# Two-layer diffusion backbone: the softmax scale moves, sign included, into the query copies; the second layer's gate products move to other steps

## The chip, the cores and the metric

One core of a Trainium2 chip runs the whole program. The time is device microseconds of one execution, as the median of several. The engines are TensorE (PE in the profile; its weight loads are PEld), VectorE (DVE), ScalarE (ACT), GpSimd (POOL) and SyncE (SP, which issues most of the transfers).

## What is computed

Two trunk layers over 512 latent and 128 context tokens, model width 1024, all in float32. Each layer normalises and modulates its input by vectors made from a conditioning, projects it once, and runs three branches: multi-head latent attention (4 heads, 96 query elements each), a short convolution, and differential attention (4 heads, two softmax maps of 64 query elements each, one subtracted from the other). The branches are gated, projected out and added to the input through a modulated gate. Of the attention this is what matters here:

```python
    scale = (MLA_NOPE + MLA_ROPE) ** -0.5
    ...
        s = (jnp.einsum('bqhd,bkhd->bhqk', qf[..., :MLA_NOPE], k_nope_f)
             + jnp.einsum('bqhr,bkr->bhqk', qf[..., MLA_NOPE:], krope_f))
        p = jax.nn.softmax(s * scale, axis=-1)
    ...
    scale = DIFF_QK ** -0.5
    ...
        s = jnp.einsum('bqhad,bkhad->bhaqk', qb.astype(jnp.float32), k_f) * scale
        p = jax.nn.softmax(s, axis=-1)
        a = p[:, :, 0] - lam_full * p[:, :, 1]
    ...
    mod = jax.nn.silu(cond) @ p['ada_w'] + p['ada_b']
    shift, scale, gate = jnp.split(mod, 3, axis=-1)
    ...
    x = x + gate * (mix @ p['w_out'])
```

## The kernel before

Activations lie transposed: 128 features on the partitions, 640 tokens (512 latent, 128 context) along the free dimension, in two halves of 320. Matrix products of float32 accuracy are made of three matmuls on a high and a low part (`mm3`, L359 to L364).

In each layer a generator `main()` makes the input projection unit by unit (`proj`, L515; 15 units of weights) and hands its results on. While it runs, the attention is made in units: for each of four heads of the differential branch one context unit of 128 queries and keys and four latent units of 128 queries and 640 keys (`diff_unit`, L599), then the same for the latent branch (`mla_unit`, L869). The function `adv` (L1043) advances `main()` by a step, then the helpers that wait in a list, then counts the step in `cnt`. At chosen steps it also advances `side()`, a generator that makes the modulation vectors still missing: a tile of weights is loaded (`at`, L148), and two products with a sum each (L153), one for each conditioning, fold it into a column. Two products and their load are called a pair here. In layer one `side()` makes the gate of this layer and shift and scale of the next, 48 pairs; in layer two only the gate, 16 pairs in two halves of 8. The second half begins with `silu_bcast` (L134): two loads, a tanh on ScalarE and two operations on VectorE (L141, L142). What is left of `side()` after the units runs before or during the output projection (`out_half`, L1149), which uses the gate in L1164.

The steps for `side()` in both layers: none up to step 18, then every eighth below 44, every fourth below 126, every fifth after that.

A differential unit goes like this. Scores of both maps go to PSUM (L614, L615; L621 for context). VectorE takes the maximum of each row (L624) and multiplies both by minus the scale (L625); ScalarE makes the exponentials with this bias and the scale, and their sums (L631). VectorE then combines the two maps (L633 to L636). TensorE transposes the result (L594), ScalarE copies it out of PSUM (L596), and TensorE multiplies it with the values (L645). A unit of the latent branch does the same with one map (L886 maximum, L887 product, L889 exponential, L891 and L892 normalising, L900 transposes, L904 and L905 high and low part, L917 values). Scores and transposes take turns in two double banks of PSUM (`pps`, two buffers); projections, values and statistics have four single banks (`ppj`).

The query of the differential branch comes out of PSUM by a plain copy on ScalarE (L530 in `proj_raw`; L986 for head 0), that of the latent branch by L807.

The program is written in one order, but the tile framework orders the instructions of each engine itself, by a plan of its own, unless they are pinned.

## Time and profile before

| | |
|---|---|
| median of three runs | 833.89 us (833.1 to 834.7) |
| the profiled execution | 832.23 us |
| its span, first to last instruction | 830.2 us |
| mean granted share of TensorE's clock | 0.992 |
| PE, PEld, DVE, ACT, POOL busy | 783.8, 739.3, 633.4, 445.8, 70.0 us |

The span is counted from the first instruction of the program. Layer one's attention runs from about 75 to 376 us, its output projection to about 440; layer two's attention runs from about 480 to 752 us. A wait is named by the instruction that waited and by what ended its wait.

### The profile page before, as it was taken

How to read it: one execution, taken by the hardware profiler on the slowest of the kernel's cores; microseconds unless marked ns; L12 is line 12 of the kernel's file. 1: busy time of each engine (PE TensorE's matmuls, PEld its weight loads, DVE VectorE, ACT ScalarE, POOL GpSimd, SP SyncE). 2: the span in 40 equal slices, each digit the busy share in tenths (PEclk: the TensorE clock that was granted, in tenths of full speed). 3: DMA queues.
4: the chain of work that ended last, by engine and by line, in shares of the span. 5: the costliest groups of instructions: out<-in, count | busy, mean ns of one | idle time of the engine just before them, and what ended most of it. 6: DMA issues, size and time to landing. Idle time of an engine off the chain costs nothing.

```text
span 830.2 us, 14320 instructions
## 1 busy us (share of the span) xinstructions
PE 783.8 (94%) x5390; PEld 739.3 (89%) x5390; DVE 633.4 (76%) x1494; ACT 445.8 (54%) x978; POOL 70.0 (8%) x45
## 2 busy tenths in 40 slices
PE   6999999989999899999999999999999899999994
PEld 1389988989999888999999998899999899899994
DVE  4788989989998778789567778987778556668535
ACT  2255447454747667674334545546557667756310
POOL 3300011030001102000220002003000200200000
PEclk9999999999999999999999999999999999999997
DMA  8916434132420322135620433411111001111503
GB/s 311 386 66 197 131 104 135 44 92 71 157 83 27 107 90 83 45 120 184 240 102 22 154 103 109 143 30 58 51 59 52 26 26 52 51 53 50 179 1 126
DMA packets 66164, 85.52 MB, mean 103 GB/s; under 512 B 4976, under 2 KB 47408, under 8 KB 66096
## 3 DMA queue, kind: packets, MB, share of 16 engines
q1 hardware_dynamic: 65520, 83.96, 30.9%
q8 instruction: 42, 0.69, 0.3%
q10 hardware_dynamic: 576, 0.66, 0.2%
q14 instruction: 26, 0.21, 0.1%
HBM read 78.14 MB, written 6.46 MB: 102 GB/s over the span
## 4 chain that ended last, share of the span: by engine, by line
PE 60%; DVE 18%; ACT 9%; DMA 7%; issue 3%; POOL 1%; SPq 1%; POOLq 0%; DVEq 0%; ACTq 0%
PE wo L363 5%; PE wo L362 4%; PE wo L364 4%; DVE jk L153 4%; DVE sm L624 2%; ACT E L631 2%; PE O L645 2%; PE p1c L362 2%; PE p1c L364 2%; PE p1c L363 2%; PE tpm L900 2%; PE p1qk L363 2%; PE p1qk L362 2%; PE S L614 2%; PE p1qk L364 2%
## 5 line engine op out<-in xcount | busy, mean ns | idle before, releaser
L153 DVE CUSTOM_DVE_ANT_0 jk<-at,cb 128x512 bf16<-128x512 f32 x128 | 91.9, 718 | 4.9 <-DMA at<-in_adaT 4.2
L631 ACT ACTIVATE E<-S,sm 128x640 f32<-128x640 f32 (+1 forms) x80 | 56.0, 706 | 61.4 <-DVE sm L625 43.3
L363 PE MATMUL wo<-mx,who 128*128 128x320 f32 x256 | 79.3, 311 | 0.1
L364 PE MATMUL wo<-mx,wlo 128*128 128x320 f32 x256 | 79.0, 309 | 0.0
L362 PE MATMUL wo<-mx,who 128*128 128x320 f32 x256 | 78.5, 310 | 0.0
L624 DVE TENSOR_REDUCE sm<-S 128x1 f32<-128x640 f32 (+1 forms) x80 | 55.3, 711 | 3.4 <-PE S L615 2.4
L889 ACT ACTIVATE Em<-Sm,smm 128x640 f32<-128x640 f32 (+1 forms) x40 | 28.3, 708 | 41.9 <-DVE smm L887 40.5
L236 ACT ACTIVATE sqn<-xn 128x320 f32<-128x320 f32 x32 | 15.1, 471 | 64.8 <-DVE xn L1164 64.5
L363 PEld LDWEIGHTS wo<-mx,who 128*128 128x128 f32 x256 | 48.1, 188 | 0.8 <-DVE mx L274 0.6
L614 PE MATMUL S<-kh,qs 128*128 128x320 f32 x128 | 40.7, 327 | 8.5 <-ACT E L631 8.4
L364 PEld LDWEIGHTS wo<-mx,wlo 128*128 128x128 f32 x256 | 48.1, 188 | 0.0
L362 PEld LDWEIGHTS wo<-mx,who 128*128 128x128 f32 x256 | 47.8, 188 | 0.0
L362 PE MATMUL v<-whi_dv,hh 128*128 128x272 f32 x160 | 46.3, 289 | 0.0
L363 PE MATMUL v<-wli_dv,hh 128*128 128x272 f32 x160 | 46.0, 288 | 0.0
L364 PE MATMUL v<-whi_dv,hl 128*128 128x272 f32 x160 | 46.0, 288 | 0.0
L645 PE MATMUL O<-v,atd 128*128 128x128 f32 x336 | 44.1, 275 | 0.2 <-ACT atd L596 0.2
L1164 DVE SCALAR_TENSOR_TENSOR xn<-wo,mod,xn 128x320 f32<-128x320 f32 (+2 forms) x48 | 19.6, 435 | 31.2 <-PE wo L364 21.4
L645 PEld LDWEIGHTS O<-v,atd 128*128 128x128 f32 x336 | 42.1, 192 | 0.5 <-ACT atd L596 0.5
L363 PE MATMUL p0qk<-hl,whi_qk 128*128 128x320 f32 x128 | 40.2, 315 | 2.4 <-DVE hl L394 2.4
L326 POOL TENSOR_TENSOR wli_c<-ri_c,whi_c 128x1024 fp32r<-128x1024 f32 x8 | 19.8, 2475 | 264.7 <-PE p0zm L363 85.4
L362 PE MATMUL p1c<-hh,whi_c 128*128 128x320 f32 x128 | 41.6, 325 | 0.0
L362 PE MATMUL p0c<-hh,whi_c 128*128 128x320 f32 x128 | 41.2, 322 | 0.0
(377 smaller groups left out, 2660.6 us busy)
## 6 DMA issues: line engine op xcount, KB each, us to landing
at<-in_adaT SPq DMA_DIRECT2D x64, 256.0 KB, 4.0
ada<-in_adaA SPq DMA_DIRECT2D x32, 256.0 KB, 5.1
ri_qk<-in_wi SPq DMA_DIRECT2D x16, 512.0 KB, 4.8
ri_c<-in_wi SPq DMA_DIRECT2D x16, 512.0 KB, 4.0
ro<-in_wo SPq DMA_DIRECT2D x16, 512.0 KB, 4.4
ri_dv<-in_wi SPq DMA_DIRECT2D x8, 544.0 KB, 4.6
ri_zd<-in_wi SPq DMA_DIRECT2D x8, 512.0 KB, 3.7
x<-in_xT SPq DMA_DIRECT2D x16, 160.0 KB, 4.8
```

Of the source, the lines that this page charges most:

```text
L153: V.tensor_tensor_reduce(out=junk, in0=raw, in1=cb2[:, c, :], scale=1.0, scalar=0.0, op0=ALU.mult, op1=ALU.add, accum_out=acc)
L326: eng.tensor_tensor(out=lo, in0=raws[hf], in1=hi.bitcast(F32), op=ALU.subtract)
L362: TE.matmul(ps, ah, bh, start=first, stop=False)
L363: TE.matmul(ps, ah, bl, start=False, stop=False)
L364: TE.matmul(ps, al, bh, start=False, stop=last)
L614: TE.matmul(ps[:, j, 0:HB], qs[:, a, qc], kh[:, a, js], start=True, stop=False)
L624: V.tensor_reduce(out=sm[:, a:a + 1], in_=Sv[a], axis=AX.XY if u < 4 else AX.X, op=ALU.max)
L631: S.activation(ev, Sv[a], AF.Exp, bias=sm[:, 2 + a:3 + a], scale=DIFF_SCALE, accum_out=so)
L645: TE.matmul(po[:, 0:128], at[:, c * 128:(c + 1) * 128], vv[:, h * 128:(h + 1) * 128], start=c == 0, stop=c == n - 1)
L889: S.activation(e if u < 4 else e[:, 0:128], Sv, AF.Exp, bias=sm[:, 1:2], scale=MLA_SCALE, accum_out=sm[:, 2:3])
L900: TE.transpose(tp[:, c * 128:(c + 1) * 128], toktile(e, c), ident)
L1164: V.scalar_tensor_tensor(out=xn[kt][:, a:e], in0=ps[:, a - j * HB:e - j * HB], scalar=mod[l][2][:, kt, c:c + 1], in1=xn[kt][:, a:e], op0=A ...
```

## The change

The scale of the softmax, with a minus sign, goes into the copies that bring the queries out of PSUM: those of the differential branch are multiplied by minus one eighth, those of the latent branch by minus one over the root of 96. Scores are then negative multiples; the row maximum becomes a row minimum, and the minimum itself is the bias of the exponential, whose scale is -1. L625 and L887 vanish. L634 becomes an operation with a tensor as its third input instead of a second scalar. The keys that are also an output are copied as before.

The steps of `side()` come from one table per layer. Layer one has the intervals of before, but the bound of step 44 is now inclusive, so that step 44 falls under "every eighth". Layer two has no step up to 50, then every twelfth. After the units the rest of layer two's `side()` runs as before.

```diff
--- before.py
+++ after.py
@@ -72,9 +72,9 @@
 
     NBLK, NW = 37, 11
     PU = ("qk2", "cq1", "c01", "c11")
-    QD, QM, SIDE0 = 5, 3, 18
-    C1, C2 = 44, 126
-    SIDES = (8, 4, 5)
+    QD, QM = 5, 3
+
+    SIDES = (((18, None), (44, 8), (126, 4), (9999, 5)), ((50, None), (9999, 12)))
 
     def slot(name, dt=F32, shape=(P, T)):
         return blk.tile(list(shape), dt, tag="blk", name=name, bufs=NBLK, padded_shape=[P, T + 4])
@@ -523,11 +523,17 @@
                     yield
             return ps
 
-        def proj_raw(nm, b, js=(0, 1), r=None):
-            r = r or slot("raw%d%s%d" % (l, nm, b))
-            for j in js:
+        def copy(dst, src, scale=None):
+            if scale is None:
+                S.copy(dst, src)
+            else:
+                S.activation(dst, src, AF.Copy, scale=scale)
+
+        def proj_raw(nm, b, scale=None):
+            r = slot("raw%d%s%d" % (l, nm, b))
+            for j in range(2):
                 ps = yield from proj(nm, b, j)
-                S.copy(r[:, j * HB:(j + 1) * HB], ps)
+                copy(r[:, j * HB:(j + 1) * HB], ps, scale)
                 yield
             return r
 
@@ -580,7 +586,7 @@
         def qk_head(h):
             nm = "qk%d" % h
             res = r["qk%d" % h] = {}
-            res["qr"] = q = yield from proj_raw(nm, 0)
+            res["qr"] = q = yield from proj_raw(nm, 0, -DIFF_SCALE)
             bg.append(q_post(h, q, res))
             res["kr"] = k = yield from proj_raw(nm, 1)
             bg.append(k_post(h, k, res))
@@ -620,19 +626,19 @@
                     own = slice(a * 64, a * 64 + 64)
                     TE.matmul(ps[:, a * 512:a * 512 + 128], ctxv(q)[own], ctxv(k)[own], start=True, stop=True)
                     Sv.append(ps[:, a * 512:a * 512 + 128])
+
             for a in range(2):
-                V.tensor_reduce(out=sm[:, a:a + 1], in_=Sv[a], axis=AX.XY if u < 4 else AX.X, op=ALU.max)
-            V.tensor_scalar(out=sm[:, 2:4], in0=sm[:, 0:2], scalar1=-DIFF_SCALE, scalar2=None, op0=ALU.mult)
+                V.tensor_reduce(out=sm[:, a:a + 1], in_=Sv[a], axis=AX.XY if u < 4 else AX.X, op=ALU.min)
             E = []
             for a in range(2):
                 e = slot("E%d" % a + tg)
                 ev = e if u < 4 else e[:, 0:128]
                 so = s0[:, u:u + 1] if a == 0 else sm[:, 5:6]
-                S.activation(ev, Sv[a], AF.Exp, bias=sm[:, 2 + a:3 + a], scale=DIFF_SCALE, accum_out=so)
+                S.activation(ev, Sv[a], AF.Exp, bias=sm[:, a:a + 1], scale=-1.0, accum_out=so)
                 E.append(e)
             V.reciprocal(sm[:, 6:7], sm[:, 5:6])
-            V.tensor_scalar(out=sm[:, 7:8], in0=s0[:, u:u + 1], scalar1=sm[:, 6:7], scalar2=neglam[:, l:l + 1],
-                            op0=ALU.mult, op1=ALU.mult)
+            V.scalar_tensor_tensor(out=sm[:, 7:8], in0=s0[:, u:u + 1], scalar=sm[:, 6:7], in1=neglam[:, l:l + 1],
+                                   op0=ALU.mult, op1=ALU.mult)
             V.scalar_tensor_tensor(out=E[0][:, 0:nk], in0=E[1][:, 0:nk], scalar=sm[:, 7:8], in1=E[0][:, 0:nk],
                                    op0=ALU.mult, op1=ALU.add)
             yield "T"
@@ -804,7 +810,7 @@
                         mm3(ps, [x[:, m * 128:(m + 1) * 128] for x in ws[b]], [x[:, js] for x in cs[b]],
                             first=b == 0, last=b == 1)
                     yield
-                    S.copy(qp[m][:, js], ps)
+                    copy(qp[m][:, js], ps, -MLA_SCALE)
                 if m == 2:
                     yield from rope(qp[2], qp[2], cosm, sinm, SWAP8, "qp%d" % l)
             r["cq"] = qp
@@ -883,10 +889,9 @@
             else:
                 TE.matmul(ps[:, 0:128], ctxv(qm), kc[:, h, :], start=True, stop=True)
                 Sv = ps[:, 0:128]
-            V.tensor_reduce(out=sm[:, 0:1], in_=Sv, axis=AX.XY if u < 4 else AX.X, op=ALU.max)
-            V.tensor_scalar(out=sm[:, 1:2], in0=sm[:, 0:1], scalar1=-MLA_SCALE, scalar2=None, op0=ALU.mult)
+            V.tensor_reduce(out=sm[:, 0:1], in_=Sv, axis=AX.XY if u < 4 else AX.X, op=ALU.min)
             e = slot("E" + tg)
-            S.activation(e if u < 4 else e[:, 0:128], Sv, AF.Exp, bias=sm[:, 1:2], scale=MLA_SCALE,
+            S.activation(e if u < 4 else e[:, 0:128], Sv, AF.Exp, bias=sm[:, 0:1], scale=-1.0,
                          accum_out=sm[:, 2:3])
             V.reciprocal(sm[:, 3:4], sm[:, 2:3])
             S.activation(e[:, 0:nk], e[:, 0:nk], AF.Copy, scale=sm[:, 3:4])
@@ -983,7 +988,7 @@
                             next(rg)
                     yield
                 for b in range(2):
-                    S.copy(raws[b][:, js], ps[b])
+                    copy(raws[b][:, js], ps[b], -DIFF_SCALE if b == 0 else None)
                 if j == 0:
                     vt, krt = values_start()
                     yield from values(0, (0,), vt, krt)
@@ -1047,7 +1052,8 @@
                 if l > 0 or cnt[0] >= 4:
                     step_bg()
                 cnt[0] += 1
-                if cnt[0] > SIDE0 and cnt[0] % SIDES[0 if cnt[0] < C1 else 1 if cnt[0] < C2 else 2] == 0:
+                every = next(n for end, n in SIDES[l] if cnt[0] <= end)
+                if every and cnt[0] % every == 0:
                     next(sg, None)
 
         def until(nm):
@@ -1136,7 +1142,7 @@
             flush()
         assert not waiting
         while "gate" not in r:
-            next(sg)
+            next(sg, None)
 
 
         while bg:
```

## Rows read from the trace of the kernel before

**Rows 1.** Page, part 1: busy us (share), instructions of each engine.

```profile
PE 783.8 (94%) x5390; PEld 739.3 (89%) x5390; DVE 633.4 (76%) x1494; ACT 445.8 (54%) x978; POOL 70.0 (8%) x45
```

**Rows 2.** Busy time by stage: stretch, length, busy us by engine, PEclk, DMA.

```profile
75.00:260.00 185.00, 176.67 (x1265) 171.68 (x1263) 170.54 (x410) 109.14 (x264) 12.34 (x7) 1.00 0.33 108
260.00:376.00 116.00, 110.03 (x761) 104.44 (x760) 88.87 (x221) 76.45 (x159) 10.07 (x4) 1.00 0.28 88
480.00:565.00 85.00, 80.47 (x562) 78.06 (x560) 74.04 (x168) 47.07 (x116) 6.76 (x3) 0.98 0.30 95
565.00:650.00 85.00, 84.36 (x604) 82.61 (x605) 65.84 (x151) 53.70 (x133) 5.39 (x5) 1.00 0.17 53
650.00:752.00 102.00, 97.73 (x687) 94.23 (x685) 60.77 (x144) 66.35 (x133) 9.73 (x4) 1.00 0.13 42
```

**Rows 3.** The same view, two short stretches; PEclk: share of clock granted.

```profile
520.00:525.00 5.00, 3.00 (x17) 2.71 (x16) 4.97 (x16) 3.51 (x8) 0.00 (x0) 0.87 0.21 73
525.00:530.00 5.00, 5.00 (x32) 5.00 (x31) 4.41 (x12) 1.98 (x7) 0.00 (x0) 0.79 0.35 98
```

**Rows 4.** Whom TensorE waited for: us in total, times, longest.

```profile
PE S L614 <- ACT E L631: 8.4, 6, 3.1
PE tpd L594 <- ACT E L631: 4.7, 4, 2.1
...
PE tpm L900 <- ACT Em L892: 2.5, 2, 1.5
...
PE Sm L362 <- DVE smm L887: 1.9, 2, 1.2
```

**Rows 5.** Whom ScalarE waited for, same columns.

```profile
ACT E L631 <- DVE sm L625: 43.3, 24, 3.9
ACT Em L889 <- DVE smm L887: 40.5, 28, 3.6
```

**Rows 6.** Instructions by time around 500 us: start, us, engine, line, operation.

```profile
497.19 2.79 POOL L326 TENSOR_TENSOR wli_qk<-ri_qk,whi_qk 128x1024 fp32r<-128x1024 f32 x1 [67.94 <-PE p1qk L363]
497.75 2.78 DVE L153 CUSTOM_DVE_ANT_0 jk<-at,cb 128x512 bf16<-128x512 f32 x1
...
500.46 1.54 DVE L624 TENSOR_REDUCE sm<-S 128x1 f32<-128x640 f32 x2
...
502.04 0.69 DVE L556 TENSOR_TENSOR qs<-raw1qk,qs 64x512 fp32r<-64x512 f32 x1
502.76 0.17 DVE L625 TENSOR_SCALAR sm<-sm 128x2 f32<-128x2 f32 x1
...
502.96 0.79 ACT L631 ACTIVATE E<-S,sm 128x640 f32<-128x640 f32 x1 [3.54 <-DVE sm L625]
...
503.90 0.76 PE L594 MATMUL tpd<-idw,E 128*128 128x128 f32 x5 [2.06 <-ACT E L631]
```

**Rows 7.** The same view around 520 us.

```profile
515.71 3.31 DVE L142 TENSOR_TENSOR cb<-cb,tb 128x1024 f32<-128x1024 f32 x1
...
522.62 0.41 PE L614 MATMUL S<-kh,qs 128*128 128x320 f32 x1 [2.00 <-ACT E L631]
```

**Rows 8.** Groups by line: count, busy us, mean ns of one, idle before.

```profile
L153 DVE CUSTOM_DVE_ANT_0 jk<-at,cb 128x512 bf16<-128x512 f32 x128 | 91.9, 718 | 4.9 <-DMA at<-in_adaT 4.2
...
L634 DVE TENSOR_SCALAR sm<-s,sm,neglam 128x1 f32<-128x1 f32 x40 | 10.9, 272 | 1.0
```

**Rows 9.** Two lines: count, ns (least/median/greatest), first and last start us.

```profile
L200 DVE SCALAR_TENSOR_TENSOR y_d<-w_d,y_d x8: 154/156/166, 139.8 to 661.0; 128x5 f32<-128x5 f32 x8
...
L688 ACT ACTIVATE z0zd<-p0zd x8: 432/437/448, 120.8 to 239.5; 128x320 f32<-128x320 f32 x8
```

**Rows 10.** Two of the instructions that write tile kc, same columns.

```profile
L834 ACT COPY kc<-kc x8: 258/261/264, 193.4 to 583.3; 64x128 f32<-64x128 f32 x8
L835 DVE COPY kc<-kr x2: 972/1242/1512, 173.4 to 564.4; 32x512 f32<-32x512 f32 x2
```

**Rows 11.** Instructions in order of time around 656 us: GpSimd.

```profile
655.52 4.82 POOL L326 TENSOR_TENSOR wli_c<-ri_c,whi_c 128x1024 fp32r<-128x1024 f32 x2 [83.37 <-PE p1zm L363]
```

## The prediction

> **What bounds the kernel now.** I read the busy shares first [rows 1]: the matmuls are busy 94% of the span and no other engine comes near, so an edit is worth time only where TensorE stands still or runs at its lower clock. Then the stages [rows 2]. The five rows are the attention of layer one (75 to 260 us differential, 260 to 376 latent) and of layer two (480 to 565 and 565 to 650 differential, 650 to 752 latent). Stretch less PE busy gives TensorE's idle time: 8.3, 6.0, 4.5, 0.6 and 4.3 us, 23.7 in all. VectorE is busy 92% of the first stretch, 87% of the third, but 60% of the last. Then the clock [rows 3]: it is 1.00 in all attention stretches of 5 us but these two, where TensorE had just stood still for 2.0 us [rows 7]. A share of 0.87 and 0.79 means that 26% and 42% of 5 us ran at 1.2 and not 2.4 GHz, 3.4 us in all, which lost half of that: 1.7 us.
>
> Who ends TensorE's waits [rows 4]: in the differential stages ScalarE's exponential (L631), 8.4 us before score matmuls and 4.7 us before transposes. Both need one of the two double banks of PSUM that scores and transposes share, and that exponential is the bank's last reader. In the latent stages the waits are smaller: 2.5 us of transposes and 1.9 of scores. And what the exponential waits for [rows 5] is VectorE's small product that turns the maximum into a bias: L625 43.3 us, L887 40.5 us. Most of that lies beside TensorE work. One such stall shows the pattern [rows 6]: two reductions at 500.46, then another VectorE operation (L556) put in between, the product at 502.76, the exponential at 502.96, and TensorE, idle for 2.06 us, goes on at 503.90. So the order on VectorE is a planner's, not the program's, and a bias that needs a further VectorE operation waits for whatever stands ahead of it.
>
> **The change part by part.** *The bias product goes.* 40 L625 (0.17 us in [rows 6]) and 40 L887 vanish from VectorE, and each exponential now waits for one reduction. The bias of map 0 is a column of its own, so I expect the first exponential to start after the first reduction. That the planner keeps regions of one tile apart is shown by tile kc: VectorE writes its partitions 64 to 95 at 173.4 us, ScalarE the others only at 193.4, though the program has them in the other order [rows 10]. In [rows 6] the first reduction ends about 501.2 (half of 1.54), the exponential could start some 0.2 later (502.96 is 0.2 behind 502.76), so it comes 1.6 us earlier of a 2.06 us stall.
>
> I went through the ten differential stalls in this way, each giving the smaller of the stall and the advance. For transposes the bank is freed by the first exponential, which gains the second reduction as well; all 4.7 us go (1.6, 0.8, 2.1, 0.2). For score matmuls after a context unit the bank is freed by the second one, which gains only the product and what stands ahead of it: 0.75, 0.9, 2.4, 0.2 in layer one, and 2.0, 0.4 in layer two, 6.6 of 8.4. Together 11.3 us, 6.6 in layer one and 4.7 in layer two. In the latent stages only the product's own 0.14 us or so goes from each of some eight stalls: 1.0 us. The rest of their wait is another chain (the transposed weights' low part, L905).
>
> *The products of layer two.* I count 228 steps of the loop in either layer. Before, sixteen pairs of products (L153) with their loads ran at steps 24 to 92; now at 60, 72 and so on to 228 are fifteen, nine in the differential part and six in the latent part, and the sixteenth comes after the loop. In [rows 6] a product that stands beside a GpSimd operation takes 2.78 us ahead of the reductions, and in [rows 7] the 3.31 us multiplication of the second half's conditioning stands ahead of the next ones. Taking these away gives no second gain in the stalls above (they are counted whole), but makes those two sure even if the exponentials start late; and with them goes the clock loss of 1.7 us.
>
> Where they go to they cost. For the latent part I compare layer one, with a pair at every fifth step (fourteen pairs, 6.0 us idle), and layer two with none (4.3 us): 0.12 us a pair, 0.7 for six. For the differential part, 4.5 us idle with some twelve pairs against 0.6 with none [rows 2]: 0.32 a pair, 2.9 for nine; as early exponentials cover a part of it, I take half, 1.5. The multiplication with its two loads moves to step 156; I take 0.7, as for six pairs. Sum 2.9; the bounds are 0 (VectorE has room) and 12.6, if all of six pairs (six times 1.44, [rows 8] give 0.72 for one) and 4.0 for the multiplication and its helper stood on TensorE's path. 2.9 is nearer to the measured prices of a pair. The loads move on SyncE's queue behind the weights of the convolution; a tile is needed only a few steps after its issue, so I cost that at nothing; if a pair came late, VectorE alone would wait, with the reductions of one unit behind it. The sixteenth pair and the gate's last sums stand before the output projection. There the projection fills four PSUM banks before it needs the gate; each takes 24 matmuls, at 0.14 us (84.36 us for 604, [rows 2]) 3.4 us, so some 13 us of cover: nothing.
>
> *Layer one's steps.* The new table keeps the intervals, but step 44 no longer counts: every pair comes one step later, and one more falls into the output projection. 1.4 us of VectorE's work leaves its fullest stretch. Gain or loss below 1 us; I take none.
>
> *Query copies.* 28 copies of 320 columns become scaled activations. Such a copy then takes what a scaled activation from PSUM of this shape takes, 0.437 us [rows 9]; all 28 are 12 us of ScalarE already, mostly paid as plain copies, and ScalarE is at most 66% busy in these stages [rows 2], so nothing. *L634* becomes a product of three tensors: 0.27 before [rows 8], as little as 0.156 by the nearest small operation of the new kind [rows 9]; 40 times 0.1 us of VectorE; on TensorE's path I take nothing, with bounds of 0 and 1 us gained (the ten stalls, 0.1 each).
>
> The Trainium skill, SBUF — State Buffer, section Who interferes with whom, says that a VectorE operation with two SBUF inputs is held while a GpSimd operation reads SBUF. The 2.78 us of [rows 6] agree with that. By this rule the new L634, now with two such inputs, could be held too, by up to a GpSimd operation; but L636 right behind it has two already, so it would only be held earlier, and the sum stays.
>
> The sum: 11.3 + 1.0 + 1.7 - 2.9 = 11.1 us. The profiled execution took 832.2 us (span 830.2 and 2.0 around it), which gives 821.1; it lay 1.7 us under the median of the runs, 833.9, so I predict 822.8 us, 1.3% faster. If all idle time of the five stages and the clock loss went, it would be 25.4 us and 808.5.
>
> **The rivals.** *VectorE takes over.* With 92% busy in layer one's first stretch, a reduction that comes late takes the place of the exponential that came late, and the planner orders everything anew. For it: the reductions themselves are queued (1.54 us behind a product in [rows 6]). Against: the 0.6 us of idle time at 77% busy in the fourth row of [rows 2]. Half of the gain, 14.0 less 7.0 less 2.9: 829.8 us.
>
> *It packs better.* The freed banks let the latent stages and waits that I left alone shrink too; half of the other idle time, some 6 us more: 817.
>
> *It doesn't do what it says.* If regions of the small tile were not kept apart, or the planner put the exponentials behind both reductions, only the product's own time and what stands ahead of it went, and layer two's moved products cost as much as they give: no change, 833.9.
>
> *The moved products decide (slower).* In layer two's latent part one unit's reduction, exponential, reciprocal, normalising, transposes and low part follow one another, and a pair put into that chain delays TensorE by its whole time. There are two stretches in which GpSimd computes 4.8 us without a break [rows 11]; a product there would be held as in [rows 6]. Price: 12.6 us as above, and two pairs held for 4.8: 22.2 against 14.0. It decides from the point where the moved products cost more than 14.0, some five times the 2.9 that I took. Result 842; in part, 837. The Trainium skill, in the section named above, states just this holding for the whole GpSimd operation; the rows show it in layer two's differential part only. Against it: the planner puts pairs where VectorE has room, which in that stage is 40% of the time.
>
> **How the numbers follow.** Forecast (818 to 828) 0.54; VectorE takes over (827 to 832) 0.19; better packed (812 to 818) 0.10; no change 0.07; slower 0.10. A measurement of this kernel tells about 0.2% from no change, 1.7 us. Faster by more than that has 0.83, within it 0.07, slower 0.10. The range leaves out the slower case and the outer parts of two others: 814 to 832.
>
> **What would show it.** After, ScalarE's wait before L631 falls from 43 us to under 25, TensorE's before L614 and L594 from 13.1 us to about 3; first exponentials start ahead of second reductions' ends. Idle time in 75 to 260 falls from 8.3 to some 2, in the first half of layer two's differential part from 4.5 to about 1, with the clock at 1.00 throughout; the latent part of layer two keeps its 4 us or rises by one. Wrong would be: exponentials that wait for both reductions; VectorE's reductions waiting on TensorE no more but TensorE on them (L624 or L905 as releaser with over 10 us); new clock drops; the first L1164 of layer two waiting for the gate long enough to stop the matmuls.

## The result and the profile after

The changed kernel takes 825.5 us (median of 4 runs, 824.7 to 827.1), 0.988 of the time before, with a 95% interval of 0.984 to 0.991: 1.2% faster. The forecast was 822.8 us and 814 to 832. Run once more beside other kernels it took 825.6 us, ratio 0.987 [0.985, 0.989]. The profiled execution took 825.7 us with a span of 823.9, 6.3 us below the span before. That execution before had a mean granted clock of 0.992, as high as any on record for its kernel (25 others: 0.978 to 0.992, mean 0.986), and the one after 0.989, the mean of its kernel; so the two spans differ by less than the medians do.

The lines moved by six or so: the reductions are now L631 (L624 before), the differential exponential L637 (L631), its score matmuls L620 and L621, transposes L600 (L594), the product of three tensors L640 (L634), the latent reduction L892 and exponential L894. L625 and L887 are gone.

The page's first part, the stretches of [rows 2], and four of 5 us, two of them those of [rows 3]:

```profile
PE 785.5 (95%) x5390; PEld 741.3 (90%) x5390; DVE 622.1 (76%) x1414; ACT 449.9 (55%) x978; POOL 68.9 (8%) x45
...
75.00:260.00 185.00, 181.47 (x1300) 177.26 (x1298) 166.99 (x392) 114.49 (x273) 11.71 (x7) 0.99 0.34 108
260.00:376.00 116.00, 108.87 (x744) 102.94 (x743) 86.91 (x200) 75.90 (x153) 10.28 (x4) 1.00 0.30 92
480.00:565.00 85.00, 83.88 (x606) 82.36 (x605) 67.22 (x139) 51.23 (x125) 11.66 (x7) 1.00 0.21 67
565.00:650.00 85.00, 83.48 (x599) 81.82 (x597) 67.11 (x148) 56.49 (x135) 3.65 (x2) 1.00 0.20 63
650.00:752.00 102.00, 97.90 (x673) 94.15 (x674) 68.23 (x148) 66.29 (x129) 5.89 (x3) 0.98 0.20 63
...
130.00:135.00 5.00, 5.00 (x25) 4.73 (x24) 3.21 (x6) 3.04 (x6) 0.00 (x0) 0.69 0.01 3
520.00:525.00 5.00, 5.00 (x36) 5.00 (x36) 4.29 (x14) 3.05 (x8) 0.00 (x0) 1.00 0.80 253
525.00:530.00 5.00, 5.00 (x39) 5.00 (x38) 3.91 (x8) 2.55 (x9) 0.00 (x0) 1.00 0.00 0
650.00:655.00 5.00, 2.88 (x7) 2.35 (x8) 4.06 (x13) 0.84 (x3) 1.10 (x1) 0.70 0.34 105
```

TensorE's idle time fell from 8.3 to 3.5 us in the first stretch and from 4.5 to 1.1 in the third. The low clock of [rows 3] is gone, but 0.69 stands at 130 us and 0.70 at 650 us, where the kernel before had 1.00. Whom TensorE and ScalarE waited for, as in [rows 4] and [rows 5]:

```profile
PE S L620 <- ACT E L637: 4.6, 3, 2.6
PE Sm L362 <- ACT Em L894: 3.7, 4, 1.3
PE vm L823 <- DVE vm L828: 3.3, 2, 2.3
PE tpm L600 <- ACT Em L897: 1.3, 1, 1.3
...
PE tpd L600 <- ACT E L637: 0.6, 1, 0.6
...
ACT E L637 <- DVE sm L631: 41.7, 34, 5.2
ACT Em L894 <- DVE smm L892: 37.7, 27, 3.5
```

The stops of [rows 4] for the differential exponential fell from 13.1 to 5.2 us. The idle time of a stretch with fixed ends mixes stages, since these begin earlier now. So here is the length of each stage in every profile of this study, in us, one execution each, from the trace's first score matmul of the differential part (S), first of the latent part (Sm) and first output projection (wo) of either layer; "between" goes from layer one's wo to layer two's S, and the last column is the span. Every kernel is told below; a2_again is the changed kernel once more. The rows of e1_soft, e2_steps and e6_diff_only are of executions with the lowest granted clock of all of that kernel (0.976, 0.975, 0.979), 2 to 5 us longer than its median.

| kernel | differential 1 | latent 1 | between | differential 2 | latent 2 | span |
|---|---|---|---|---|---|---|
| before | 172.3 | 111.9 | 107.0 | 168.4 | 109.9 | 830.2 |
| after | 167.4 | 113.9 | 105.8 | 163.1 | 111.9 | 823.9 |
| a2_again | 167.9 | 113.7 | 105.8 | 163.3 | 112.0 | 824.3 |
| e1_soft | 169.5 | 116.9 | 105.9 | 168.1 | 109.0 | 830.8 |
| e2_steps | 173.3 | 117.2 | 108.2 | 165.9 | 112.7 | 839.4 |
| e3_second | 169.5 | 113.0 | 105.9 | 161.1 | 112.3 | 824.0 |
| e4_split | 168.2 | 115.6 | 106.8 | 162.6 | 111.0 | 826.8 |
| e5_step44 | 168.6 | 115.9 | 105.9 | 162.8 | 112.1 | 826.4 |
| e6_diff_only | 168.4 | 121.3 | 108.4 | 162.9 | 112.6 | 836.2 |
| e7_every6 | 167.8 | 113.5 | 105.8 | 168.5 | 108.9 | 824.4 |
| e8_c01 | 167.7 | 113.8 | 105.7 | 162.3 | 108.7 | 820.8 |
| e9_noc | 167.4 | 107.1 | 106.6 | 162.3 | 106.6 | 810.2 |
| e10_diff_noc | 166.3 | 108.4 | 106.8 | 162.3 | 107.5 | 813.3 |
| e11_before_noc | 174.2 | 108.4 | 106.9 | 168.2 | 105.7 | 824.3 |

The change took 4.9 and 5.3 us out of the differential parts and put 2.0 us into each latent part. Both of these were to be explained.

The stall of [rows 6] is gone. The same place in the trace after, start and length in us:

```profile
502.29 1.54 DVE L631 TENSOR_REDUCE sm<-S 128x1 f32<-128x640 f32 x2
...
503.14 0.79 ACT L637 ACTIVATE E<-S,sm 128x640 f32<-128x640 f32 x1 [2.15 <-DVE sm L631]
...
503.92 0.79 ACT L637 ACTIVATE E<-S,sm 128x640 f32<-128x640 f32 x1
...
504.13 0.60 PE L600 MATMUL tpd<-idw,E 128*128 128x128 f32 x4
```

The two reductions end at 503.83; the first exponential starts at 503.14, ahead of the second one's end, and TensorE goes on to the transposes without a stop. Of the 40 pairs of exponentials 30 have the first one start before the second reduction's end; in the trace before it was none. What is left of the stops is one at 129 us, with the low clock behind it:

```profile
126.34 0.68 DVE L153 CUSTOM_DVE_ANT_0 jk<-at,cb 128x512 bf16<-128x512 f32 x1
...
126.95 0.28 DVE L631 TENSOR_REDUCE sm<-S 128x1 f32<-128x128 f32 x1
127.15 0.68 DVE L153 CUSTOM_DVE_ANT_0 jk<-at,cb 128x512 bf16<-128x512 f32 x1
...
127.76 0.28 DVE L631 TENSOR_REDUCE sm<-S 128x1 f32<-128x128 f32 x1
...
128.44 0.36 ACT L637 ACTIVATE E<-S,sm 128x128 f32<-128x128 f32 x1
...
128.94 0.41 PE L620 MATMUL S<-kh,qs 128*128 128x320 f32 x1 [2.57 <-ACT E L637]
```

Here products of the gate stand ahead of and between the two short reductions of a context unit; TensorE stops until the second exponential has read the bank. The other is at 652 us:

```profile
646.28 4.83 POOL L326 TENSOR_TENSOR wli_c<-ri_c,whi_c 128x1024 fp32r<-128x1024 f32 x2 [84.94 <-PE p1zm L363]
...
648.93 2.19 DVE L197 TENSOR_TENSOR w_d<-y_d 128x5 f32<-128x5 f32 x1
651.16 0.17 DVE L198 TENSOR_TENSOR w_d<-w_d,e 128x5 f32<-128x5 f32 x1
...
651.64 0.42 DVE L828 TENSOR_TENSOR vm<-vm,vm 128x256 fp32r<-128x256 f32 x1
...
652.12 1.22 PE L823 MATMUL vm<-wuv,ckA 128*128 128x256 f32 x2 [2.29 <-DVE vm L828]
```

A VectorE operation on 128x5 elements lasts 2.19 us, until GpSimd has done; the next ones of its size take 0.17. The low parts of the values (L828) are queued behind it, and TensorE waits for them. This stop is not new. The kernel before has it too, behind the GpSimd stretch of [rows 11], with the clock at 1.00 behind it:

```profile
661.15 1.13 PE L817 MATMUL vm<-wuv,ckA 128*128 128x256 f32 x4 [2.08 <-DVE vm L822]
```

New is only the lower clock behind it, and that makes most of the 2.0 us in layer two's latent part. Nearly the whole of that part before (first row) and after:

```profile
649.00:759.00 110.00, 105.73 (x744) 102.22 (x743) 67.56 (x158) 73.21 (x149) 9.73 (x4) 1.00 0.14 42
640.00:752.00 112.00, 107.73 (x745) 103.52 (x744) 73.92 (x161) 73.55 (x148) 9.54 (x4) 0.98 0.19 60
```

TensorE is idle for 4.3 us in either; a clock of 0.98 of 112 us, and more exactly 0.70 and 0.96 in the ten us from 650, is 1.7 us by the prediction's reckoning.

### The profile page after: what moved, and what is told of

It is laid out like the page before. It is cut to its first block, busy times and chain, and to the rows that moved or that the text cites. A ratio compares the mean times of both kernels' runs of the same rounds, so it can differ in the third digit from the quotient of the medians.

```text
span 823.9 us, 14193 instructions
## 1 busy us (share of the span) xinstructions
PE 785.5 (95%) x5390; PEld 741.3 (90%) x5390; DVE 622.1 (76%) x1414; ACT 449.9 (55%) x978; POOL 68.9 (8%) x45
## 4 chain that ended last, share of the span: by engine, by line
PE 70%; DVE 13%; DMA 7%; ACT 5%; issue 3%; POOL 1%; SPq 0%; POOLq 0%; DVEq 0%; ACTq 0%
PE wo L363 4%; PE wo L364 4%; PE wo L362 4%; PE O L651 3%; DVE jk L153 2%; PE v L362 2%; PE v L364 2%; PE v L363 2%; PE S L620 2%; PE p1qk L363 2%; PE p1qk L362 2%; PE tpm L905 2%; PE p1qk L364 2%; PE p1c L362 2%; PE p1c L363 2%
## 5 line engine op out<-in xcount | busy, mean ns | idle before, releaser
L153 DVE CUSTOM_DVE_ANT_0 jk<-at,cb 128x512 bf16<-128x512 f32 x128 | 89.6, 700 | 8.7 <-DMA at<-in_adaT 7.7
L637 ACT ACTIVATE E<-S,sm 128x640 f32<-128x640 f32 (+1 forms) x80 | 56.5, 709 | 45.5 <-DVE sm L631 41.7
L631 DVE TENSOR_REDUCE sm<-S 128x1 f32<-128x640 f32 (+1 forms) x80 | 55.0, 711 | 5.4 <-PE S L621 5.0
L894 ACT ACTIVATE Em<-Sm,smm 128x640 f32<-128x640 f32 (+1 forms) x40 | 28.3, 708 | 39.0 <-DVE smm L892 37.7
L620 PE MATMUL S<-kh,qs 128*128 128x320 f32 x128 | 40.6, 327 | 5.4 <-ACT E L637 4.6
L326 POOL TENSOR_TENSOR wli_c<-ri_c,whi_c 128x1024 fp32r<-128x1024 f32 x8 | 19.8, 2477 | 267.9 <-PE p1zm L363 84.9
L362 PE MATMUL p0qk<-hh,whi_qk 128*128 128x320 f32 x128 | 39.6, 320 | 1.4 <-ACT hh L390 1.4
```

What stands on the lines that cost most here:

```text
L153: V.tensor_tensor_reduce(out=junk, in0=raw, in1=cb2[:, c, :], scale=1.0, scalar=0.0, op0=ALU.mult, op1=ALU.add, accum_out=acc)
L326: eng.tensor_tensor(out=lo, in0=raws[hf], in1=hi.bitcast(F32), op=ALU.subtract)
L362: TE.matmul(ps, ah, bh, start=first, stop=False)
L620: TE.matmul(ps[:, j, 0:HB], qs[:, a, qc], kh[:, a, js], start=True, stop=False)
L631: V.tensor_reduce(out=sm[:, a:a + 1], in_=Sv[a], axis=AX.XY if u < 4 else AX.X, op=ALU.min)
L637: S.activation(ev, Sv[a], AF.Exp, bias=sm[:, a:a + 1], scale=-1.0, accum_out=so)
```

## The experiments

All were timed in five rounds, beside the kernel before on the same chip; ratios are to it, with 95% intervals. e1 to e4 shared one chip (before: 835.6 us), e6 to e8 and the second run of the changed kernel another (836.2), e5 and e9 to e11 a third (836.3).

**The two parts of the change alone.** e1_soft has the new softmax and the steps of before:

```
-    SIDES = (((18, None), (44, 8), (126, 4), (9999, 5)), ((50, None), (9999, 12)))
+    SIDES = (((18, None), (43, 8), (125, 4), (9999, 5)), ((18, None), (43, 8), (125, 4), (9999, 5)))
```

> The softmax part alone, with the steps of the kernel before in both layers. My theory (each exponential starts behind its own reduction, which shortens the wait for a bank of PSUM, in both layers): layer one as in the changed kernel, some 4 us earlier at the start of layer two, and in layer two some 3 us more, as the products still delay reductions there; 828 us (826 to 830) against 834.3 before. Rival (the step table brings the gain): 831 us or more.

Measured 830.5 us (827.7 to 832.6), ratio 0.9925 [0.9898, 0.9953]. Between the two theories. e2_steps is the kernel before with the new table alone (the line with + of the change's diff, and the condition that reads it in `adv`):

> The step table alone, with the softmax of the kernel before. My theory: layer one unchanged within 1 us; layer two's differential part loses its two stalls of 2 us and the 1.7 us of the low clock, and pays some 2 us later: 831 us (829 to 833). Rival one (the table is worth nothing without early exponentials): 834 to 836. Rival two (the table brings the gain): 827 or less.

Measured 837.7 us (834.0 to 843.3), ratio 1.0025 [0.9998, 1.0051]: the table alone brings nothing, as rival one had it. So the parts do not add up to the whole: -5.1 and +2.1 us by medians, together -8 to -11. In layer two's differential part the softmax alone gains 0.3 us, the steps alone 2.5, both 5.3; either part alone leaves a stop there, of 3.84 us at 522 us in e1_soft and of 2.40 at 512 in e2_steps. And both are longer in layer one's latent part, by 5.0 and 5.3 us, where the whole change is longer by 2.0. That part after, in e1_soft and in e2_steps:

```profile
257.00:371.00 114.00, 107.11 (x740) 101.74 (x739) 83.57 (x194) 73.96 (x149) 10.28 (x4) 1.00 0.28 85
...
260.00:377.00 117.00, 110.38 (x740) 105.97 (x741) 85.67 (x193) 73.98 (x150) 9.96 (x4) 0.96 0.28 83
...
264.00:381.00 117.00, 109.97 (x735) 104.92 (x735) 88.48 (x213) 73.28 (x149) 10.43 (x4) 0.96 0.27 82
```

TensorE idles equally long, 6.9, 6.6 and 7.0 us. What differs is the clock, by some 5 us. It does so over all executions too. Span times mean granted clock is an estimate of the span with the lower level taken out (it counts all of the lost share as lost time); averaged over the executions of each kernel it is 822.5 us before (clock 0.986), 814.1 for e1_soft (0.983), 821.0 for e2_steps (0.982) and 814.1 for the changed kernel beside later runs (0.989). By it the softmax alone brings the whole 8.4 us and the steps alone 1.5; that the medians do not add up is the clock, lower than before with either part alone and higher with both.

**Early start or missing product.** e3_second lets the first exponential wait for the second reduction as well, with no small product (the bias of map 0 is then the other map's minimum, a different shift of the same softmax):

```
-                S.activation(ev, Sv[a], AF.Exp, bias=sm[:, a:a + 1], scale=-1.0, accum_out=so)
+                S.activation(ev, Sv[a], AF.Exp, bias=sm[:, 1:2], scale=-1.0, accum_out=so)
```

> As the changed kernel, but both exponentials of a differential unit take the minimum of the second map as bias (any bias cancels in the softmax), so none can start before the second reduction; there is no product. My theory (the early start is what counts): half or more of the softmax part's gain is lost, 829 us (827.5 to 831), with more transposes and scores waiting for exponentials. Rival (the missing product counts): within 1.5 us of the changed kernel, 825 to 827.

Measured 823.4 us (822.1 to 826.1), ratio 0.9849 [0.9815, 0.9882]. My theory falls: the early start is not needed. e4_split is the opposite, e2_steps with the product split so that each map has its own right behind its reduction:

```
-            V.tensor_scalar(out=sm[:, 2:4], in0=sm[:, 0:2], scalar1=-DIFF_SCALE, scalar2=None, op0=ALU.mult)
+                V.tensor_scalar(out=sm[:, 2 + a:3 + a], in0=sm[:, a:a + 1], scalar1=-DIFF_SCALE, scalar2=None, op0=ALU.mult)
```

> The changed kernel's step table, the softmax of before, but the product of a differential unit split in two, one right behind each reduction, so that the first exponential can start early though the product is there. My theory (early start counts): 827.5 us (826 to 829), near the changed kernel. Rival (the missing product counts): no faster than the table alone, 830 to 833, since VectorE has 40 operations more.

Measured 831.8 us (827.2 to 835.3), ratio 0.9945 [0.9918, 0.9971], 5.9 us under e2_steps. By the time that is the rival's range, by the distance to the table alone it is not. In the trace the median time from the end of the first reduction to its exponential is 1.9 us in e2_steps, 0.9 in e4_split, 0.8 in e3_second and 0.04 after. The differential parts of e4_split (168.2 and 162.6 us) are as short as those of the changed kernel (167.4 and 163.1), and those of e3_second nearly (169.5 and 161.1). The kernel with the same latent part and no product in the differential one is e6_diff_only below; its ratio is 0.9959 [0.9938, 0.9980], no different. So with the new steps about 1 us of advance is enough: by one operation less behind the second reduction, or by a product behind each. The last 0.8 us buys nothing more.

But e4_split has a second difference: its products are 128x1, that of e2_steps is 128x2. Of e2_steps:

```profile
505.57 5.16 POOL L325 TENSOR_TENSOR wli_qk<-ri_qk,whi_qk 128x1024 fp32r<-128x1024 f32 x2 [67.98 <-DVE sm L623]
...
508.55 2.20 DVE L624 TENSOR_SCALAR sm<-sm 128x2 f32<-128x2 f32 x1
...
511.73 0.77 PE L593 MATMUL tpd<-idw,E 128*128 128x128 f32 x5 [2.40 <-ACT E L630]
```

The product is held until GpSimd has done, 2.20 us instead of 0.17, and TensorE stops behind it; four of the 40 in e2_steps take 0.56 to 2.20. Of the 80 in e4_split, nine of which began beside a GpSimd operation, none took over 0.16. How much of the 5.9 us is the advance and how much the hold is not shown; the changed kernel has neither product.

**The step of 44.** e5_step44 undoes the shift in layer one:

```
-    SIDES = (((18, None), (44, 8), (126, 4), (9999, 5)), ((50, None), (9999, 12)))
+    SIDES = (((18, None), (43, 8), (125, 4), (9999, 5)), ((50, None), (9999, 12)))
```

> The change with layer one's steps exactly as before: the pair of step 44 stays at every fourth step's count and is not shifted. Theory one, that the shift is worth nothing: as the changed kernel, 825.6 us, ratio 0.987 to 0.988. Theory two, that the shifted pair is what stands ahead of the reductions near 129 us, where TensorE stops 2.7 us and the granted clock is 0.69 from 130 to 135 us: both go, 822 us, ratio 0.983.

Measured 828.4 us (826.1 to 830.0), ratio 0.9898 [0.9871, 0.9926]: neither; undoing it costs. The stop at 129 us is longer, one product more stands ahead of the two reductions, and the granted clock is 0.66 behind it as well. Of e5_step44, the same matmul as above:

```profile
130.04 0.41 PE L620 MATMUL S<-kh,qs 128*128 128x320 f32 x1 [4.24 <-ACT E L637]
```

The shift is worth some 2.8 us by the medians, of which 1.2 lie in that stage. The intervals of this ratio and of the changed kernel's (0.985 to 0.989 in its second run) overlap, so its size stays open. Span times clock is 814.0 us here and 814.1 in the changed kernel's second run: by that estimate all of the 2.8 us is clock (0.985 against 0.989).

**The latent part.** The changed kernel again, and e6_diff_only, in which the latent queries are copied plainly, and maximum, small product (here L893) and scale are back:

```
-                    copy(qp[m][:, js], ps, -MLA_SCALE)
+                    copy(qp[m][:, js], ps)
-            V.tensor_reduce(out=sm[:, 0:1], in_=Sv, axis=AX.XY if u < 4 else AX.X, op=ALU.min)
+            V.tensor_reduce(out=sm[:, 0:1], in_=Sv, axis=AX.XY if u < 4 else AX.X, op=ALU.max)
+            V.tensor_scalar(out=sm[:, 1:2], in0=sm[:, 0:1], scalar1=-MLA_SCALE, scalar2=None, op0=ALU.mult)
```

> The changed kernel once more, unaltered, so that the runs beside it have it as their neighbour. Every theory expects the ratio that it had the first time, 0.988 (between 0.984 and 0.992).

> The change without its latent part: there the query copies are plain, the maximum and the small product are back, and the exponential scales. The latent stages of the changed kernel's profile are longer than before by 2.0 us in layer one and 2.0 us in layer two. Theory one, that the latent part's own edits do this (scaled query copies take longer on ScalarE, and exponentials that come earlier fall behind the cast of the next hidden tile there): both stages get their time back, 822 us and a ratio near 0.984. Theory two, that these stages lose by what lies elsewhere (stalls that the order of the work happens to give, falls of the granted clock): no gain from undoing it, and the 40 small products come back on VectorE; 826 to 827 us, ratio 0.988 to 0.991.

The first gave 825.6 us (822.9 to 826.3), 0.9869 [0.9849, 0.9890]; e6_diff_only 833.4 (830.1 to 838.2), 0.9959 [0.9938, 0.9980]. Neither theory allowed for this: the latent part's edits, for which I had taken 1.0 us, are worth 7.8. By the estimate used above (817.5 against 814.1 us) 3.4 of it is work and waiting, the rest the clock (0.983 against 0.989). Layer one's latent part is 121.3 us long in the profile of e6_diff_only, its longest execution, with two stops of 2.6 and 3.4 us and granted clocks of 0.50 to 0.84 behind them. The second one:

```profile
325.09 2.82 POOL L326 TENSOR_TENSOR wli_c<-ri_c,whi_c 128x1024 fp32r<-128x1024 f32 x1
325.62 2.98 DVE L861 TENSOR_TENSOR kml<-krf,kmh 32x640 fp32r<-32x640 f32 x1
...
329.04 0.28 DVE L892 TENSOR_REDUCE smm<-Sm 128x1 f32<-128x128 f32 x1
329.24 0.81 DVE L911 TENSOR_TENSOR plm<-tpm,phm 128x640 fp32r<-128x640 f32 x1
...
329.97 0.14 DVE L893 TENSOR_SCALAR smm<-smm 128x1 f32<-128x1 f32 x1
...
330.11 0.63 PE L362 MATMUL Sm<-kmh,qmh 96*128 96x320 f32 x1 [3.44 <-DVE smm L893]
```

The key's low part (L861, 0.82 us where it is not held) is held by GpSimd, which is done at 327.9, and ends at 328.6; the reduction comes after it, and a product of 0.14 us lies 0.65 us behind the reduction because L911 stands in between. In the trace after, the reduction of the same unit ends at 321.6 and its exponential starts at once; the hold and the stop are there too, but shorter:

```profile
322.12 0.41 PE L362 MATMUL Sm<-kmh,qmh 96*128 96x320 f32 x1 [1.16 <-ACT Em L894]
```

So 0.8 of the 3.4 us are the product's, and the rest is where GpSimd's stretch fell.

**Where the pairs stand.** e7_every6 issues layer two's pairs at every sixth step from 50, all by step 150:

```
-    SIDES = (((18, None), (44, 8), (126, 4), (9999, 5)), ((50, None), (9999, 12)))
+    SIDES = (((18, None), (44, 8), (126, 4), (9999, 5)), ((50, None), (9999, 6)))
```

> The change with layer two's pairs at every sixth step from 50, so that the sixteen pairs are issued by step 150, nearly all of them in the differential part, and none in the latent part. Theory one, that pairs in the latent part cost it its 2 us in layer two: 824 us, ratio 0.986. Theory two, that the differential part is where VectorE's time is short (its products there delay reductions and evictions) and the latent part has room: the differential part of layer two loses 2 to 4 us, 828 us, ratio 0.991.

Measured 827.9 us (826.2 to 829.3), ratio 0.9902 [0.9882, 0.9922]. Both theories are right in part: layer two's latent part is 3.0 us shorter, but its differential part 5.4 longer, with one stop of 3.9 us at 558 us behind products of 1.5 us each. This gives prices of a pair: 0.5 us for each of the six in the latent part, 0.8 for each of the seven more in the differential part. But 1.7 us of either difference is the lower clock, behind the stop at 652 us after and the one at 558 us here; the stop at 652 us stands in e7_every6 as well (2.28 us at 656.8), with no lower clock behind it. Without that it is 0.2 and 0.5 us a pair.

**GpSimd's blocks.** GpSimd computes the low parts of some weight blocks (L326). e8_c01 gives one of the two of the latent parts to VectorE, e9_noc both:

```
-    PU = ("qk2", "cq1", "c01", "c11")
+    PU = ("qk2", "cq1")
```

> The change with one of GpSimd's four products of the stream combination, c01, computed on VectorE. In the changed kernel's profile a VectorE operation of 128x5 at 648.9 us took 2.19 us beside a GpSimd product of 4.8 us; TensorE then stood 2.6 us at 652 us, and its granted clock was 0.70 from 650 to 655 us. Theory one, that the hold by GpSimd is the cause: stall and fall of the clock go, 2 to 4 us less, 822 to 824 us, ratio 0.983 to 0.986, where the move of the product adds 1 to 2 us of VectorE's time beside other work. Theory two, that another GpSimd product takes the place of c01 beside the same operation, or that VectorE is late by the moved product: 826 to 828 us, ratio 0.988 to 0.991.

> The change with both c01 and c11, the low parts of two weight blocks of the latent part's hidden tiles, taken from GpSimd and given to VectorE (c01 is such a low part too; the earlier expectation called it a product of the stream combination, which it isn't). With c01 alone moved the run gave 820.1 us, and its profile keeps a stop of TensorE of 3.0 us at 327.8 us with granted clocks of 0.92 and 0.74 in the ten us there, and one of 1.6 us at 703.1 us, both a few us behind GpSimd's stretches at 315.5 and 697.1 us. Theory one, that GpSimd's stretches cause these as well: both go, 3 to 5 us less, 816 to 817 us, ratio 0.976 to 0.978. Theory two, that these stops come from the order of the work on VectorE, which gets another 5 us of products: 820 to 822 us, ratio 0.981 to 0.984.

(The edit of e9_noc; e8_c01 keeps "c11". c01 and c11 are weight blocks of the latent part's hidden tiles, as the second text has it.)

e8_c01 took 820.1 us (818.5 to 822.6), ratio 0.9812 [0.9790, 0.9834], more than theory one allowed for; e9_noc 812.6 (811.9 to 813.8), 0.9715 [0.9687, 0.9743], the fastest of all, 13 us under the changed kernel. In e8_c01 the operation that took 2.19 us takes 0.17 and the stop and the low clock at 650 us are gone; here are that operation and its stretch of 5 us:

```profile
649.76 0.17 DVE L197 TENSOR_TENSOR w_d<-y_d 128x5 f32<-128x5 f32 x1
...
650.00:655.00 5.00, 4.85 (x29) 4.26 (x29) 4.33 (x14) 3.46 (x8) 0.00 (x0) 1.00 0.52 145
```

In e9_noc the latent parts are 6.8 and 5.3 us shorter than after, though VectorE has 8 operations of 1.2 us more there, for 8 of 2.4 us that GpSimd has no more. Two stretches of e9_noc, nearly the whole of the two latent parts:

```profile
255.00:364.00 109.00, 107.24 (x753) 103.14 (x752) 83.56 (x199) 75.39 (x157) 0.00 (x0) 1.00 0.30 89
630.00:740.00 110.00, 109.23 (x771) 105.83 (x770) 75.73 (x171) 75.95 (x156) 0.00 (x0) 1.00 0.20 61
```

TensorE idles 1.8 and 0.8 us there, the clock stays at 1.00. I had expected 3 to 5 us; it is 7.5 under e8_c01.

**What the change is worth without these blocks.** e10_diff_noc is e6_diff_only, and e11_before_noc the kernel before, both with the same line as e9_noc:

> The change without its latent part (maximum and small product back there), and with c01 and c11 on VectorE. Beside GpSimd's blocks the latent part's edits were worth 7.8 us: 833.4 against 825.6 us. Theory one, that the small product was dear because GpSimd's stretches hold VectorE ahead of it: without these stretches the undone latent part costs little, at most 2 us over the kernel with the whole change and the same blocks moved, 817 to 820 us, ratio 0.978 to 0.982. Theory two, that one more step in each of 40 chains from reduction to exponential costs by itself, wherever GpSimd is: again 6 to 8 us over it, 823 to 826 us, ratio 0.984 to 0.988.

> The kernel before, with nothing of the change, and with c01 and c11 on VectorE. Theory one, that the change brings its time mostly by taking small products off VectorE where GpSimd holds it: without these stretches much less is left for it, and this kernel comes within 5 us of the change with the same blocks moved, 820 to 824 us, ratio 0.981 to 0.986. Theory two, that the change's worth and GpSimd's blocks add up: 9 us over that kernel, 826 to 829 us, ratio 0.988 to 0.991.

e10_diff_noc took 816.3 us (815.4 to 818.0), 0.9760 [0.9731, 0.9789]; e11_before_noc 826.2 (824.6 to 826.5), 0.9869 [0.9844, 0.9895]. So the latent part's edits are worth 3.7 us without these blocks and 7.8 with them: about half of their worth needs GpSimd's blocks beside them, and half is there anyway; each theory has a part. That the other half is held operations that no longer delay a further one is argued from the stop above and not shown; by the estimate of span times clock 1.6 of the 3.7 us and 4.7 of the 7.8 are the lower clock. The second result is against theory one and just on theory two's edge: the change as a whole is worth no less where these blocks do not hold VectorE (826.2 to 812.6, 13.5 us) than where they do (8 to 11); that it is worth more is not clear of the noise. Moving the blocks alone brings 10 us, the change alone 8 to 11, and both 23.7.

## Why the prediction was right, and where its steps were not

**The differential stalls (11.3 us, right in size).** Expected were 6.6 us in layer one and 4.2 in layer two (4.7 and 1.7 of clock, less 2.2 for what moves there); the stages became 4.9 and 5.3 us shorter. Between e11_before_noc and e9_noc, with c01 and c11 on VectorE in both, it is 6.8 and 5.9. One step of the working failed: that the stops before transposes go because the first exponential starts after the first reduction. It does start there, as [rows 10] suggested, but e3_second takes that start away and loses nothing that can be measured. That the term came out in size, though the early start counted in it was not needed, is in part luck. As far as the runs tell, what counts is 1 us less from reduction to exponential, a product that GpSimd can no longer hold (L625 took 1.11 us at 174.98 us, ahead of the longest stop of [rows 4]), and that the 2.78 and 3.31 us operations of [rows 6] and [rows 7] no longer stand there; e1_soft, which has the products in their old places, gains only 0.3 us in layer two.

**The latent stalls (1.0 us, wrong in size and sign).** The stages grew by 2.0 us each, where -0.5 and, with six pairs, +0.2 were expected. In layer two 1.7 of the 2.0 us is the lower clock behind a stop that was there before, which the prediction, with its one clock loss, had no term for. The six pairs there make a difference of 2.8 us (e2_steps against before) to 3.0 (after against e7_every6), but 1.7 of each is this clock; 1.1 to 1.3 is left for the pairs, where I had taken 0.7. And e8_c01, with the pairs where the change has them but without the held operation, needs 108.7 us for this part, no more than e7_every6 without a pair in it. GpSimd's blocks, whose cost I left as it was, were mis-sized: they cost 3.5 and 4.2 us in the kernel before (against e11_before_noc) but 6.8 and 5.3 after (1.7 of the latter that clock); that the new order put other operations beside them is seen in the stops above. Without these blocks the change does to the latent parts -1.3 and +0.9 us, near what was forecast. That this part of layer one is 5 us or more longer in e1_soft, e2_steps and e6_diff_only is mostly clock, 5 to 7 us of it in their three profiles, so it shows no such effect of the edits. Which held operations make the 2.0 us of that part after was traced only in the stops above.

**The clock (1.7 us, right at its place and given back elsewhere).** 520 to 530 us has 1.00 now. The lower level at 130 and at 650 us cost, worked out as in the prediction, 5 times 0.31 and 5 times 0.30, 3.1 us in all. But the 1.7 us were read from an execution with as high a clock as the kernel before ever showed. Over the executions beside a2_again the mean granted clock is 0.986 before and 0.989 after, some 3 us in the change's favour by the same reckoning.

**The moved products decide (a rival).** Its place was right, its price not. One product of layer two's latent part fell beside a GpSimd stretch, in the trace after:

```profile
699.87 4.87 POOL L326 TENSOR_TENSOR wli_c<-ri_c,whi_c 128x1024 fp32r<-128x1024 f32 x2 [48.77 <-PE p1c L363]
...
702.51 2.78 DVE L153 CUSTOM_DVE_ANT_0 jk<-at,cb 128x512 bf16<-128x512 f32 x1
...
705.86 0.33 PE L600 MATMUL tpm<-idw,Em 128*128 128x128 f32 x1 [1.34 <-ACT Em L897]
```

It was held for 2.1 us of its 2.78 and stopped TensorE for 1.3, not for 4.8.

**Signs that misled.** ScalarE's wait for the reductions was to fall under 25 us and is 41.7. It only has another releaser: an engine that is busy 55% has to wait for something, and of these 41.7 us TensorE saw 5.2. The stops of TensorE were the sign to go by: 13.1 to 5.2, forecast 3.

**The small terms.** Step 44, taken as nothing, may be worth up to 2.8 us, all of it clock by the estimate above. L640 was to fall from 0.27 to 0.16 us; its median is 0.22, and three of the 40 were held and took 2.03 us at 496.5 us and some 0.93 at 171.9 and 554.7, with no stop of TensorE there, as the prediction had it for the rule in the Trainium skill (SBUF — State Buffer, section Who interferes with whom). The same rule names operations with two SBUF inputs as held; L197, L661, L861 and L640 have two and were. But L625 and L624 of e2_steps have one and were held too, as 128x2; as 128x1 none of the 17 such products that began beside a GpSimd operation in the traces before and of e2_steps, e4_split and e6_diff_only took over 0.16 us. The gate's last sums cost nothing: at the output projection of layer two TensorE stops for 0.2 us. The scaled query copies were not tried by themselves.

Over all: by the two profiles 6.3 us of span where 11.1 were forecast. Of the 4.8 that are missing, 4.3 are the latent stages' (4.0 longer, forecast 0.3 shorter); the differential ones gave 10.2 of 10.8, with the lower clock at 130 us already in them. By the medians, in which the clock before is the usual one, the change gave 8.4 to 10.6 us.

## What to carry to other kernels

Look for what shares a port or a queue with the chain before you cost an edit by its own duration: a 0.15 us operation in 40 chains was worth 3.7 us in one kernel and 7.8 in its neighbour, by what GpSimd did beside it, and about half of both was time at the lower clock. A helper engine that takes work off a VectorE with room (here 67 and 75% busy in these stages) can cost more than the work: moving 8 operations of 2.4 us back was worth 13 us. And price a moved operation by an experiment that moves it, with the clock taken out: two stages differed by 0.5 us a pair, and more than half of that was the lower level behind a stop that both kernels have. Each execution's mean granted clock stands beside its span; look at it before you explain a difference between two profiles.

## What the runs showed of the hardware

One kernel's time follows the clock that its execution was granted, on the same chip: of 25 runs of the kernel before, the one with a mean of 0.992 took 831.7 us and the one with 0.978 took 841.3, 0.7 us for each 0.001. The spread of a kernel's runs is mostly this: a straight line by the clock takes three quarters of the variance of the 25.

The same stop of TensorE is followed by the low level in one kernel and not in the next. At 129 us e9_noc stops for 2.57 us and e10_diff_noc for 2.72, with a stretch before it that is equally empty; the 5 us behind differ:

```profile
125.00:130.00 5.00, 2.23 (x15) 1.73 (x15) 4.93 (x17) 4.30 (x12) 0.00 (x0) 1.00 0.35 128
130.00:135.00 5.00, 5.00 (x26) 5.00 (x25) 3.18 (x7) 2.82 (x5) 0.00 (x0) 0.66 0.01 3
...
125.00:130.00 5.00, 2.28 (x20) 2.05 (x19) 4.93 (x15) 4.64 (x13) 0.00 (x0) 1.00 0.60 214
130.00:135.00 5.00, 4.81 (x33) 4.55 (x32) 4.43 (x11) 3.53 (x8) 0.00 (x0) 1.00 0.01 3
```

The first two rows are of e9_noc (0.66, 26 matmuls started), the last two of e10_diff_noc (1.00, 33 started). So such a stop has two prices, its own and in some executions a stretch at the lower clock, 1.7 us here and 3.4 behind the 3.84 us stop of e1_soft at 522 us. Whether the second comes could not be told from these traces beforehand.

GpSimd holds small VectorE operations too: a 128x5 one took 2.19 us instead of 0.17, and the 128x2 product up to 2.20 in e2_steps. In the nine cases in e4_split the same product as 128x1 was not held.
